# The low parts of fifteen weight tiles move from POOL to DVE in a hybrid attention block

## The chip, the cores and the metric

One core of a Trainium2 chip runs the kernel. The metric is the device time of one execution in microseconds (us); a lower time is better. The kernel before was run three times: 841.33 us median, 840.12 to 841.64.

## The reference, cut to what matters

A decoder block on a sequence of 256 tokens and width 2048 (batch 1, float32): an adaLN-modulated norm, one large input projection, two causal token mixers side by side, a projection for each mixer, a gated merge, an output projection and a sandwich norm.

```python
ada = c @ w_ada + b_ada
shift, scale, gate = split(ada, 3)
h = rms_norm(x, g_pre) * (1 + scale) + shift
proj = h @ w_in                                   # 2048 x 11824
ya = (oa * silu(za)) @ w_br_a                     # 1024 x 2048, oa: sparse attention, 16 heads
yb = (ob * silu(zb)) @ w_br_b                     # 1024 x 2048, ob: dilated attention, 8 heads
merged = sigmoid(ma) * ya + sigmoid(mb) * yb
out = merged @ w_out                              # 2048 x 2048
return x + gate * rms_norm(out, g_post)
```

## The kernel before

Every product with a large weight runs in three parts: a weight tile and an activation are each split into a high part in TensorE's own 32-bit format (fp32r) and a low part, the rest, and high x high, high x low and low x high are summed in PSUM. A weight travels like this. `dma` (L459) loads one item, a tile `raw` of 128 x 1024, from the SP queue; seven such buffers exist. `prep` (L471) makes the high part `wH` with a copy on ACT (L477) and the low part `wL = raw - wH` with a subtraction (L479). There are three buffers of each. `main` (L541) then issues the matmuls through `product` (L518): L535 (wH by the activation's high part), L536 (wH by its low part), L538 (wL by its high part). For an item of two 128-row blocks by 512 columns that is twelve matmuls of 512 columns, six for each half of the tokens.

The items are a list in a fixed order. First come four passes of the input projection; they are not touched by the change. Then come the 32 items of the two branch products (kind `w`, key `br`; four panels of 512 columns, for each panel four items of `w_br_a` and four of `w_br_b`). 32 items of kind `gate` are spread over the end of the projection and over the branch products. A gate item is a 128 x 1024 tile of `w_ada` that DVE multiplies by a column of c and adds to a running sum `gacc` (the first of each half in L497, the others in L499); it has no matmul. Last come the 32 items of the output product (key `out`). `prep` runs three items ahead of `main` (AHEAD).

After the last item of a branch panel, `evac` (L587) merges it on DVE: L619 scales the PSUM result by the gate of its mixer, once for each half of the tokens, and, for the second branch, L622 adds the two mixers' results into `MA`. TensorE then turns that panel's `MA` (L1090, `m_ps`) so that it can be the activation of the output product, ACT and DVE write its high and low parts (L1096, L1097). The gate's sum gets its bias on POOL (L1117), is split and broadcast by TensorE (L1123, L1124) and used at L634 and in the final rows (L1174 to L1188).

The framework's scheduler puts each engine's instructions in order when the program is built, and then every engine works through its own list. That order is not always the order of the source: a loop that writes L619, L622, L619, L622 can be found with another instruction of DVE between its two lines.

The change concerns L478 and L479: `on_pool` is true for an item of kind `w` that doesn't belong to the input projection and whose number in the list is divisible by four. For those, L479 is issued on POOL.

Of the kernel before, what the change touches and what calls it, by code (L numbers as in the profile page):

```python
# [9 lines left out]
F32 = mybir.dt.float32  # L10
# [4 lines left out]
OP = mybir.AluOpType  # L15
# [31 lines left out]
def _build(ctx, tc, x, c, positions, w_ada, b_ada, g_pre, g_post, w_in, pe_ck, pe_cv, w_ck1, w_ck2,  # L47
           w_cv1, w_cv2, w_br_a, w_br_b, w_out, out):
    nc = tc.nc
    V, A, T, G, DMA = nc.vector, nc.scalar, nc.tensor, nc.gpsimd, nc.sync  # L50
# [155 lines left out]
    @contextmanager  # L206
    def behind(*instructions):
        with ExitStack() as st:
            for i in instructions:
                st.enter_context(tc.issue_after(i.ins))  # L210
            yield
# [216 lines left out]
    for n, p in enumerate(panels):  # L428
        a_ = FILL[1] if p[0] in FILLED else 0 if p[0] == "mb" else a
        items += w_job(w_in[0], a_, b, p[1], p[2], (xH, xL), ("proj", 3, 1, p))  # L430
        if n in (3, 4):
            for q in range(4):
                it = Item()
# [11 lines left out]
    for half in range(2):  # L445
        for kt in range(KT):
            it = Item()
# [23 lines left out]
    def prep(i):  # L471
        it = items[i]
        raw = it.raw
        if it.kind in ("w", "ck"):
            H, L = (wp.tile([128, 1024], F32R, name="w" + x, tag="w" + x, bufs=3)[:, :it.nk * it.n].rearrange(
                "p (k n) -> p k n", k=it.nk) for x in "HL")
            A.activation(H, raw, AF.Copy)  # L477
            on_pool = it.kind == "w" and it.jobs[0].key[0] != "proj" and i % 4 == 0  # L478
            (G if on_pool else V).tensor_tensor(L, raw, H.bitcast(F32), op=OP.subtract)  # L479
            it.H, it.L = H, L  # L480
            return
        if it.kind == "ada":
            if it.kt0 == 0:
                accs[it.piece] = ST[:, len(accs) % 2].rearrange("p (h n) -> p h n", h=2)
            acc = accs[it.piece][:, :, :it.n // 2]
        else:
            if it.half not in gacc:
                need("A")
                gacc[it.half] = big.tile([128, 1024], F32, name=f"gacc{it.half}", tag=("cv", "k2")[it.half])
            acc = gacc[it.half]  # L490
        with behind(*(first_h if i < 8 else ())):
            for j in range(it.nk):
                cc, r = cT[:, it.kt0 + j:it.kt0 + j + 1], raw[:, j, :]
                if it.kind == "ada":
                    r = r.rearrange("p (h n) -> p h n", h=2)
                if it.kt0 + j == 0:
                    V.tensor_scalar(acc, r, cc, None, op0=OP.mult)  # L497
                else:
                    V.scalar_tensor_tensor(acc, r, cc, acc, op0=OP.mult, op1=OP.add)  # L499
        if it.fin:  # L500
            if it.kind == "ada":
                fin_ada(it.piece)
            else:
                done.add("gate")

    def fin_ada(piece):
        def gen():
            yield
            make_h(*piece, accs[piece])
            done.add(("h", piece))  # L510
            yield
        side.insert(0, gen())

    def need(*keys):
        while not all(k in done for k in keys):
            side_step(True)
# [631 lines left out]
    def more(i):  # L1148
        prep(i)
        if nxt[0] < n:  # L1150
            dma(nxt[0])
            nxt[0] += 1
# [57 lines left out]
```

## Time and profile before

| | before |
|---|---|
| median of 3 runs | 841.33 us (840.12 to 841.64) |
| the profiled execution | 840.99 us |
| its span | 839.2 us |
| TensorE (PE) busy | 800.3 us, 95% of the span |
| VectorE (DVE) busy | 695.1 us, 83% |
| ScalarE (ACT) busy | 416.4 us, 50% |
| GpSimd (POOL) busy | 135.6 us, 16% |
| mean granted TensorE clock | 0.993 |

The time of the execution is 1.79 us longer than the span, which reaches from the first to the last instruction of the program. Matmuls are pipelined and the records of two neighbours overlap, so a busy PE says only that it has something to do; it is its holes that count here. An instruction's record on DVE or POOL starts when the engine takes it, and can hold time in which it does not yet work on data. Times in the rows are counted from the start of the span.

### The profile page before, as it was taken

To read this page: it belongs to the slowest core of one execution; us is meant where nothing else is said; L and a number is where in the kernel's file an instruction comes from. 1 tells how busy PE (TensorE), PEld (TensorE's weight loads), DVE (VectorE), ACT (ScalarE), POOL (GpSimd) and SP (SyncE) were. 2 spreads that over 40 slices of the span, in tenths; PEclk is the share of its full clock that TensorE was granted. 3 is DMA by queue.
4 is the path that set the end of the run, shared out by engine and by line. 5 is a ranking of instruction groups with operands and counts; after the bars stand their busy time and mean duration, and the time that the engine had idled before them with its cause. 6 is when DMAs were issued, how large, how long until landed. Compare 5 with 4: busy or idle time off the path is not lost.

```text
span 839.2 us, 12023 instructions
## 1 busy us (share of the span) xinstructions
PE 800.3 (95%) x4200; PEld 672.1 (80%) x4200; DVE 695.1 (83%) x1080; ACT 416.4 (50%) x671; POOL 135.6 (16%) x128
## 2 busy tenths in 40 slices
PE   5997999999999999999999999999999989999995
PEld 4785778889887778888888999888888868888884
DVE  4999999999997888898978998777676998855335
ACT  3953263343434446575766666445544433444452
POOL 4200000000000025154311110001003032122221
PEclk9999999999999999999999999999999999999998
DMA  9988899999798547844444545554589989986622
GB/s 313 369 295 262 246 311 291 366 301 325 253 337 295 160 154 227 261 137 128 137 138 116 141 134 158 170 154 145 151 292 322 338 281 324 302 294 196 191 93 100
DMA packets 106663, 193.27 MB, mean 230 GB/s; under 512 B 7561, under 2 KB 36073, under 8 KB 105961
## 3 DMA queue, kind: packets, MB, share of 16 engines
q1 hardware_dynamic: 105088, 189.17, 69.7%
q10 hardware_dynamic: 1514, 3.33, 1.2%
q8 instruction: 33, 0.54, 0.3%
q14 instruction: 28, 0.23, 0.1%
HBM read 190.38 MB, written 2.10 MB: 229 GB/s over the span
## 4 chain that ended last, share of the span: by engine, by line
PE 51%; DVE 4%; issue 1%; ACT 1%; DMA 1%; DVEq 0%; ACTq 0%
PE mm L535 13%; PE mm L536 13%; PE mm L538 13%; PE mm L530 2%; PE mm L525 2%; PE mm L527 2%; DVE wL L479 1%; PE pt_ps L901 1%; PE sA L865 1%; DVE og L1187 1%; PE pvb_ps L1035 1%; PE sB L1025 1%; PE ot_ps L925 1%; PE ot_ps L923 1%; DMA raw<-in_w_ada_dram 1%
## 5 line engine op out<-in xcount | busy, mean ns | idle before, releaser
L477 ACT ACTIVATE wH<-raw 128x1024 fp32r<-128x1024 f32 (+2 forms) x276 | 275.9, 1002 | 326.3 <-PE mm L536 184.0
L479 DVE TENSOR_TENSOR wL<-raw,wH 128x1024 fp32r<-128x1024 f32 (+2 forms) x261 | 309.4, 1191 | 82.9 <-ACT wH L477 80.4
L535 PE MATMUL mm<-wH,xH 128*128 128x512 f32 (+2 forms) x640 | 247.5, 390 | 8.7 <-DVE KB L608 2.5
L536 PE MATMUL mm<-wH,xL 128*128 128x512 f32 (+2 forms) x640 | 245.7, 386 | 0.0
L538 PE MATMUL mm<-wL,xH 128*128 128x512 f32 (+2 forms) x640 | 198.5, 387 | 0.7 <-DVE wL L479 0.6
L535 PEld LDWEIGHTS mm<-wH,xH 128*128 128x128 f32 x640 | 120.2, 188 | 35.1 <-issue 6.1
L538 PEld LDWEIGHTS mm<-wL,xH 128*128 128x128 f32 x640 | 117.7, 188 | 27.7 <-DVE wL L479 2.8
L536 PEld LDWEIGHTS mm<-wH,xL 128*128 128x128 f32 x640 | 120.4, 188 | 23.4 <-DVE xL L237 0.5
L499 DVE SCALAR_TENSOR_TENSOR ST<-raw,vecT,ST 128x768 f32<-128x768 f32 (+2 forms) x75 | 76.3, 1017 | 0.3
L525 PE MATMUL mm<-xH,wH 128*128 128x256 f32 x256 | 67.5, 284 | 1.2 <-DVE VB L608 1.2
L527 PE MATMUL mm<-xL,wH 128*128 128x256 f32 x256 | 66.9, 280 | 0.0
L479 POOL TENSOR_TENSOR wL<-raw,wH 128x1024 fp32r<-128x1024 f32 x15 | 37.6, 2510 | 130.9 <-ACT wH L477 130.9
L530 PE MATMUL mm<-xH,wL 128*128 128x256 f32 x256 | 53.6, 282 | 0.4 <-DVE wL L479 0.4
L535 PE MATMUL mm<-wH,yH 128*128 128x512 f32 x128 | 51.2, 400 | 0.0
L536 PE MATMUL mm<-wH,yL 128*128 128x512 f32 x128 | 51.0, 399 | 0.0
L536 PE MATMUL mm<-wH,mL 128*128 128x512 f32 x128 | 50.8, 397 | 0.0
L535 PE MATMUL mm<-wH,mH 128*128 128x512 f32 x128 | 50.7, 396 | 0.0
L499 DVE SCALAR_TENSOR_TENSOR gacc<-raw,vecT,gacc 128x1024 f32<-128x1024 f32 x30 | 43.9, 1464 | 7.5 <-DMA raw<-in_w_ada_dram 7.4
L525 PEld LDWEIGHTS mm<-xH,wH 128*128 128x128 f32 x256 | 48.0, 188 | 1.9 <-ACT wH L477 1.0
L527 PEld LDWEIGHTS mm<-xL,wH 128*128 128x128 f32 x256 | 48.2, 188 | 0.0
L530 PEld LDWEIGHTS mm<-xH,wL 128*128 128x128 f32 x256 | 40.1, 189 | 1.0 <-DVE wL L479 1.0
L538 PE MATMUL mm<-wL,yH 128*128 128x512 f32 x128 | 40.7, 398 | 0.0
(294 smaller groups left out, 1010.2 us busy)
## 6 DMA issues: line engine op xcount, KB each, us to landing
raw<-in_w_in_dram SPq DMA_DIRECT2D x165, 512.0 KB, 4.4
raw<-in_w_ada_dram SPq DMA_DIRECT2D x48, 512.0 KB, 5.3
raw<-in_w_ada_dram SPq DMA_DIRECT2D x48, 384.0 KB, 4.6
raw<-in_w_out_dram SPq DMA_DIRECT2D x32, 512.0 KB, 4.9
raw<-in_w_br_a_dram SPq DMA_DIRECT2D x16, 512.0 KB, 5.6
raw<-in_w_br_b_dram SPq DMA_DIRECT2D x16, 512.0 KB, 5.4
raw<-in_w_in_dram SPq DMA_DIRECT2D x29, 256.0 KB, 3.0
raw<-in_w_ada_dram SPq DMA_DIRECT2D x24, 256.0 KB, 6.0
```

Source lines behind the costliest of these rows:

```text
L477: A.activation(H, raw, AF.Copy)
L479: (G if on_pool else V).tensor_tensor(L, raw, H.bitcast(F32), op=OP.subtract)
L499: V.scalar_tensor_tensor(acc, r, cc, acc, op0=OP.mult, op1=OP.add)
L525: T.matmul(ps, lhsT=it.H[:, j, bs], rhs=sH[:, it.kt0 + j, :], start=(first and j == 0 and b == 0), stop=False, skip_group_check=True)
L527: T.matmul(ps, lhsT=it.H[:, j, bs], rhs=sL[:, it.kt0 + j, :], start=False, stop=False, skip_group_check=True)
L530: T.matmul(ps, lhsT=it.L[:, j, bs], rhs=sH[:, it.kt0 + j, :], start=False, stop=(last and j == it.nk - 1), skip_group_check=True)
L535: T.matmul(ps, lhsT=sH[:, it.kt0 + j, ts], rhs=it.H[:, j, cs], start=(first and j == 0), stop=False)
L536: T.matmul(ps, lhsT=sL[:, it.kt0 + j, ts], rhs=it.H[:, j, cs], start=False, stop=False)
L538: T.matmul(ps, lhsT=sH[:, it.kt0 + j, ts], rhs=it.L[:, j, cs], start=False, stop=(last and j == it.nk - 1))
L865: T.matmul(o, lhsT=QT[:, u.t, h // 2, h % 2, :], rhs=KTt[:, hl, :, 0:128] if u.t == 0 else KTt[:, hl, u.br, :], start=(hl == 0), stop=(hl ...
L901: T.transpose(ps[:, j, :], u.P[:, j * 128:(j + 1) * 128], ident)
L923: T.matmul(ps, lhsT=vr.rearrange("p l d -> p (l d)"), rhs=u.H[:, :, b, :], start=(first and b == 0), stop=False, skip_group_check=True)
```

## The change

The low part of every weight tile is made on DVE. `on_pool` is gone, and with it the fifteen subtractions on POOL; nothing else is edited.

```diff
@@ -475,8 +475,7 @@
             H, L = (wp.tile([128, 1024], F32R, name="w" + x, tag="w" + x, bufs=3)[:, :it.nk * it.n].rearrange(
                 "p (k n) -> p k n", k=it.nk) for x in "HL")
             A.activation(H, raw, AF.Copy)
-            on_pool = it.kind == "w" and it.jobs[0].key[0] != "proj" and i % 4 == 0
-            (G if on_pool else V).tensor_tensor(L, raw, H.bitcast(F32), op=OP.subtract)
+            V.tensor_tensor(L, raw, H.bitcast(F32), op=OP.subtract)
             it.H, it.L = H, L
             return
         if it.kind == "ada":
```

## Rows read from the trace of the kernel before

**Rows 1.** The page: busy time, share of the span and instructions of each engine, and from the costliest groups the subtraction on POOL (count, then busy us, mean ns of one, idle us before them and what ended it).
```profile
PE 800.3 (95%) x4200; PEld 672.1 (80%) x4200; DVE 695.1 (83%) x1080; ACT 416.4 (50%) x671; POOL 135.6 (16%) x128
...
L479 POOL TENSOR_TENSOR wL<-raw,wH 128x1024 fp32r<-128x1024 f32 x15 | 37.6, 2510 | 130.9 <-ACT wH L477 130.9
```

**Rows 2.** The table by stretches: from and to, length, busy us and (instructions) of PE, PE's weight loads, DVE, ACT and POOL, then the granted clock (1.00 is full), the DMA engines' share and GB/s.
```profile
680.00:685.00 5.00, 5.00 (x23) 4.03 (x22) 4.93 (x5) 1.99 (x2) 1.88 (x2) 1.00 0.64 207
685.00:690.00 5.00, 2.23 (x10) 1.50 (x8) 5.00 (x4) 1.06 (x1) 2.31 (x1) 1.00 0.92 344
690.00:695.00 5.00, 4.07 (x13) 3.33 (x14) 5.00 (x9) 1.72 (x3) 0.50 (x1) 0.66 1.00 371
720.00:730.00 10.00, 10.00 (x45) 8.16 (x44) 9.62 (x12) 4.80 (x6) 0.00 (x0) 1.00 0.90 292
```

**Rows 3.** The timeline of PE around its longest hole of the stretch, later than the start: start, us, line, operation, tiles and shapes, count, and in brackets the idle time before it and what ended it.
```profile
686.84 0.39 PE L538 MATMUL mm<-wL,yH 128*128 128x512 f32 x1
690.93 0.63 PE L1090 MATMUL m_ps<-ident,MA 128*128 128x128 f32 x4 [3.71 <-DVE MA L622]
```

**Rows 4.** The chain that ended last, followed through the stretch from 664 to 700 us: start, us, what.
```profile
678.49 4.29 DMA raw<-in_w_ada_dram
...
683.84 1.22 DVE wL L479
685.06 3.08 DVE gacc L499
...
690.11 0.69 DVE MA L622
...
691.57 0.43 PE mm L535
...
694.98 0.23 PE mm L535
```

**Rows 5.** The hole on PE in the input projection, with no POOL work near it: the timeline of PE, and the table by stretches (columns as in Rows 2).
```profile
74.94 0.47 PE L535 MATMUL mm<-wH,xH 128*128 128x512 f32 x1 [1.73 <-DVE QB L610]
```
```profile
70.00:80.00 10.00, 7.25 (x30) 4.95 (x28) 10.00 (x22) 4.88 (x6) 0.00 (x0) 1.00 0.80 237
```

**Rows 6.** The timeline of POOL from 622 us on.
```profile
646.78 2.39 POOL L479 TENSOR_TENSOR wL<-raw,wH 128x1024 fp32r<-128x1024 f32 x1 [2.64 <-ACT wH L477]
...
678.30 2.43 POOL L479 TENSOR_TENSOR wL<-raw,wH 128x1024 fp32r<-128x1024 f32 x1 [3.46 <-ACT wH L477]
683.85 3.46 POOL L479 TENSOR_TENSOR wL<-raw,wH 128x1024 fp32r<-128x1024 f32 x1 [3.12 <-ACT wH L477]
694.50 2.53 POOL L479 TENSOR_TENSOR wL<-raw,wH 128x1024 fp32r<-128x1024 f32 x1 [7.20 <-ACT wH L477]
701.21 2.41 POOL L479 TENSOR_TENSOR wL<-raw,wH 128x1024 fp32r<-128x1024 f32 x1 [4.18 <-ACT wH L477]
```

**Rows 7.** The timeline of DVE, instructions of the branch products in order of time.
```profile
613.31 0.76 DVE L497 TENSOR_SCALAR gacc<-raw,vecT 128x1024 f32<-128x1024 f32 x1 [1.34 <-DMA raw<-in_w_ada_dram]
...
638.01 1.28 DVE L499 SCALAR_TENSOR_TENSOR gacc<-raw,vecT,gacc 128x1024 f32<-128x1024 f32 x1 [2.68 <-DMA raw<-in_w_ada_dram]
...
644.06 1.23 DVE L479 TENSOR_TENSOR wL<-raw,wH 128x1024 fp32r<-128x1024 f32 x1 [2.18 <-ACT wH L477]
...
647.51 2.75 DVE L499 SCALAR_TENSOR_TENSOR gacc<-raw,vecT,gacc 128x1024 f32<-128x1024 f32 x1 [1.02 <-DMA raw<-in_w_ada_dram]
...
677.24 1.22 DVE L479 TENSOR_TENSOR wL<-raw,wH 128x1024 fp32r<-128x1024 f32 x1
678.38 2.90 DVE L497 TENSOR_SCALAR gacc<-raw,vecT 128x1024 f32<-128x1024 f32 x1
681.32 2.61 DVE L499 SCALAR_TENSOR_TENSOR gacc<-raw,vecT,gacc 128x1024 f32<-128x1024 f32 x2
...
684.98 3.42 DVE L499 SCALAR_TENSOR_TENSOR gacc<-raw,vecT,gacc 128x1024 f32<-128x1024 f32 x1
688.32 0.68 DVE L619 SCALAR_TENSOR_TENSOR MB<-MB,mm 128x512 f32<-128x512 f32 x1
688.91 1.27 DVE L499 SCALAR_TENSOR_TENSOR gacc<-raw,vecT,gacc 128x1024 f32<-128x1024 f32 x1
690.11 0.68 DVE L622 TENSOR_TENSOR MA<-MA,MB 128x512 f32<-128x512 f32 x1
...
694.91 3.21 DVE L499 SCALAR_TENSOR_TENSOR gacc<-raw,vecT,gacc 128x1024 f32<-128x1024 f32 x1
...
701.84 0.69 DVE L619 SCALAR_TENSOR_TENSOR MA<-MA,mm 128x512 f32<-128x512 f32 x1 [0.73 <-PE mm L538]
```

**Rows 8.** The load of a gate item: its issue on the SP queue, and the loads of the stretch from 676 to 692 us (count, KB each, median us from issue to landing).
```profile
682.63 0.34 SPq L467 DMA_DIRECT2D raw<-in_w_ada_dram  x1
```
```profile
raw<-in_w_ada_dram SPq DMA_DIRECT2D x5, 512.0 KB, 5.9
```

**Rows 9.** The next merge of a panel, and the output product: the timeline of DVE (L622), of PE (L1090, and the L538 that uses the tile made by POOL in the third row), and of POOL.
```profile
714.09 0.69 DVE L622 TENSOR_TENSOR MA<-MA,MB 128x512 f32<-128x512 f32 x1
```
```profile
715.11 0.60 PE L1090 MATMUL m_ps<-ident,MA 128*128 128x128 f32 x4
```
```profile
802.35 2.40 POOL L479 TENSOR_TENSOR wL<-raw,wH 128x1024 fp32r<-128x1024 f32 x1 [8.69 <-ACT wH L477]
```
```profile
807.89 0.62 PE L538 MATMUL mm<-wL,mH 128*128 128x512 f32 x2
```

## The prediction

> **What bounds the kernel now.** I read the page first. PE is busy in 95% of the span and DVE in 83%; the fifteen subtractions to be moved take 37.6 us of a POOL that has little else to do [rows 1]. On those shares alone the change looks bad: it takes work from the idle engine and gives it to the second busiest. So I read the table by stretches next, from 630 us on, where the fifteen lie. PE has no hole of note there except one: 2.23 us busy of the five from 685 to 690, and the granted clock falls to a mean of 0.66 in the five that follow [rows 2]. DVE is full in both. The timeline of PE gives the size: the last matmul before the hole begins at 686.84 and ends at 687.23, and the transposes of the merged panel (L1090) wait 3.71 us, until 690.93, for the sum in L622 on DVE [rows 3]. The chain runs through DVE there: wL, gate sum, merge, with a load in front [rows 4].
>
> The clock costs more. From 691.57 to 694.98 matmuls step by 0.43 us, afterwards by 0.23: eight steps at half speed, 1.2 instead of 2.4 GHz, 8 x 0.20 = 1.6, and four transposes of this span 0.63 instead of 0.44, together about 1.7 us [rows 3, 4]. The hole with its slow clock thus costs 3.7 + 1.7 = 5.4 us. Everywhere else in the stage PE is fed, so this is nearly all that an edit here can win. A hole of 1.73 us in the input projection cost no clock: 1.00 in its stretch [rows 5].
>
> **Why DVE is late.** I laid the timelines of POOL and DVE side by side. POOL's subtraction runs from 683.85 to 687.31; the gate sum that DVE took at 684.98 needs 3.42 us and ends at 688.40, 1.1 after POOL. The same form takes 1.27 at 688.91 [rows 6, 7]. The one from 694.91 takes 3.21 beside a POOL subtraction to 697.03, the one from 647.51 2.75 beside one to 649.17; the first of a gate half takes 2.90 from 678.38 beside one to 680.73, and 0.76 at 613.31 with POOL idle [rows 6, 7]. Four of four end about one own length after POOL ends. I read it as: DVE does no work on such an instruction while POOL works. And POOL's own 3.46 at 683.85 holds 1.06 of waiting for a DVE subtraction.
>
> The Trainium skill says the same in its page SBUF — State Buffer (Who interferes with whom): DVE and GpSimd share one pair of ports, and with two SBUF inputs on DVE the second to start is blocked until the first ends. The Trainium skill's page Perfetto Trace Analysis (Optimizing Scalar/DVE Operations) says, against this change, that with a saturated DVE some work may be moved off it, to GpSimd even; in the next sentence it warns that between these two it might not help. By the first sentence the kernel gets slower (rival 3).
>
> **What the change removes and adds.** Each moved subtraction adds one of 1.22 us to DVE, 1.14 from its start to the next start (677.24 to 678.38) [rows 7].
>
> - *Three before the full stretch* (the last is that of 646.78). DVE idles 2.68, 2.18 and 1.02 us there [rows 7]; two additions go into the first two holes, the third costs 1.14 and removes 2.75 - 1.27 = 1.48. Nothing on the path.
> - *Two in the stretch ahead of the hole* (POOL at 678.30 and 683.85). They add 2 x 1.14 = 2.28 and remove 2.90 - 0.76 = 2.14 and 3.42 - 1.27 = 2.15, together 4.29. Net 2.0 us that DVE is earlier.
> - *One or two behind it* (694.50 and 701.21). The first adds 1.14 and removes 3.21 - 1.27 = 1.94. The second adds 1.14 and blocked no DVE instruction: L619 took its ordinary 0.69 [rows 6, 7]. DVE waits 0.73 for PE at that place [rows 7] and so has room.
> - *Eight from 733 on*, the output product. POOL's wL is done at 804.75 there, 3.1 us before L538 needs it at 807.89 [rows 9]. PE has no hole; nothing changes, and on DVE the tile is ready earlier. Should that cover go, each would cost what it is late, at most 1.2.
>
> L1117 stays on POOL, and what it costs DVE is in both kernels.
>
> **The new time of the merge, step by step.** I replay DVE from 677.24 in the order it has now, with the two additions in source order. wL to 678.38; gate start 0.70 to 679.08; added wL (POOL could begin it at 678.30, so its inputs are there [rows 6]) to 680.22; two gate sums of 1.20 to 682.62; wL to 683.76; gate sum to 684.96, whose data land at 682.78 [rows 4], in time; added wL (inputs there by 683.85 [rows 6]) to 686.10; L619 to 686.70. Between L619 and L622 stands a gate sum now [rows 7], so the list is not in source order, and what will fill that place can't be read from this trace. Its load was issued at 682.63, when the buffer of the gate sum from 681.32 came free, and with the median of 5.9 it lands near 688.5 (an estimate) [rows 8]; the sum began at 688.91. In the replay that buffer is free at 681.42, so 1.2 earlier, landing 687.1 to 687.3. Then the sum ends at 688.3 to 688.5. L1090 follows L622's start by 0.82 (690.93 - 690.11). So:
>
> - nothing between: L622 at 686.74, L1090 at 687.56, hole 0.3;
> - a wL of 1.14 between: hole 1.4;
> - the gate sum between: L622 at 688.4, hole 2.0.
>
> Below zero it can't go, as the hole's start is set by PE. I take 1.3, near the middle one, since two of the three fillers are real work. Gain of the hole: 3.71 - 1.3 = 2.4. The clock: a hole of 1.73 kept it [rows 5], one of 3.71 lost it; 0.3 to 2.0 lie at or near the former, so I count the whole 1.7. Sum: 840.99 - 2.4 - 1.7 = 836.9 for a profiled execution. The median of the runs is 0.34 above the profiled one, so 837.2. The bounds 0.3 and 2.0 give 836.2 and 837.9.
>
> **What is late next.** PE comes some 4 us earlier to 701 us, DVE only 2.0 + 0.8 at that place. It has 0.73 there against the 1.14 of the last addition; then it is 9.62 of 10 busy up to 730 [rows 2]. The next merge is tight: L622 ends at 714.78, L1090 starts at 715.11 [rows 9], 0.3 of slack. A miss of 0.5 there would take back 0.5; I keep it for the range.
>
> **The rivals.**
>
> 1. *The hole only shortens and the clock falls all the same* (the gate sum in between waits longer for its load, hole 2 to 3 us). For it: the load is 5.9 us long with the DMA engines 0.92 busy [rows 2, 8]. Gain 3.71 - 2.5 = 1.2, or 840.1; with a hole of 2.0 it is 839.6. Chance 13%.
> 2. *The change does nothing here.* DVE's freed time goes into waits for gate loads: the chain shows one of 4.29 [rows 4], and whichever gate sum is first in the list holds all behind it. Or a new order of the list opens a small hole at another merge. 840.5 to 841.5. Against it: the landing at 682.78 comes before its turn in the replay. Chance 13%.
> 3. *DVE is simply full, and slower.* If the long instructions aren't POOL's doing, the two additions ahead of L622 come on top: 2 x 1.14 = 2.3, hole 6.0, 841.33 + 2.3 = 843.6. It decides at one point: whether a collision costs DVE less than the 1.14 that an addition costs. For it: DVE is full around the hole [rows 2]. Against it: 1.48, 2.14, 2.15 and 1.94 measured, each ended by POOL's end [rows 6, 7]. Chance 12%. The first sentence quoted above from the Trainium skill's Perfetto Trace Analysis would have it so; the four collisions speak for the second.
>
> **How the numbers follow.** The forecast has 62%; of rival 1 half is beyond 0.2% (1.7 us, about what a measurement of this kernel can tell from no change). Faster: 62 + 7 = 69%. Within: 6 + 13 = 19%. Slower: 12%. Likeliest 837.2; its own range is 836.2 to 837.9, widened by the runs' 1.2 below their median. The range of 8 in 10 goes from 835.4 (hole gone, lowest run) to 840.7, which takes in rival 1 and a part of rival 2 and leaves out rival 3.
>
> **What would show it.** Right: POOL has 113 instructions, DVE's gate sums at the merge of the second panel are all near 1.27 and the first of the half 0.76; L622 of that panel lies 2 us or more earlier; PE's hole before L1090 is under 2 us; the clock is 1.00 from 690 to 695. Wrong: DVE instructions of over 2 us remain where POOL has none, or L622 waits behind a gate sum whose load has not landed, or a hole before L1090 at 715 or 740. If the hole is small and the clock still falls, the step on the clock was wrong.

## The result

| | before | changed |
|---|---|---|
| median of 6 runs | 841.49 us (840.12 to 843.69) | 837.25 us (836.89 to 838.74) |
| span of the profiled execution | 839.2 us | 835.5 us |
| DVE busy | 695.1 us | 706.5 us |
| POOL busy | 135.6 us | 97.3 us |

The ratio is 0.995, with a 95% interval from 0.9935 to 0.9965. The kernel is 4.2 us faster, and DVE is busy 11.4 us more than before. Lines of the changed kernel are one less than those of before from L479 on: L478 is the subtraction, L498 the gate sum, L618 and L621 the merge, L1089 the transposes, L1116 the gate's bias.

The page of the changed kernel, busy time of each engine, and the subtraction's group, now all on DVE (count, busy us, mean ns, idle before):

```profile
PE 798.6 (96%) x4200; PEld 671.1 (80%) x4200; DVE 706.5 (85%) x1095; ACT 415.9 (50%) x671; POOL 97.3 (12%) x113
...
L478 DVE TENSOR_TENSOR wL<-raw,wH 128x1024 fp32r<-128x1024 f32 (+2 forms) x276 | 329.1, 1198 | 75.7 <-ACT wH L477 73.0
```

The table by stretches of the changed kernel, columns as in [rows 2]:

```profile
70.00:80.00 10.00, 8.27 (x29) 6.00 (x28) 10.00 (x22) 4.88 (x6) 0.00 (x0) 0.83 0.78 248
...
685.00:690.00 5.00, 3.48 (x19) 2.63 (x17) 4.71 (x7) 1.06 (x1) 0.00 (x0) 1.00 1.00 393
690.00:695.00 5.00, 5.00 (x26) 4.16 (x25) 5.00 (x8) 3.30 (x5) 0.00 (x0) 1.00 1.03 392
```

Set beside [rows 2]: PE has 3.48 busy of the five from 685 to 690 (2.23 before), and the clock is whole in the next five (0.66 before). The timeline of PE gives the hole, to be read against [rows 3]:

```profile
687.66 0.39 PE L535 MATMUL mm<-wH,yL 128*128 128x512 f32 x1
689.57 0.63 PE L1089 MATMUL m_ps<-ident,MA 128*128 128x128 f32 x4 [1.52 <-DVE MA L621]
```

1.52 us in place of 3.71, with the same releaser. And the timeline of DVE ahead of it, to be read line by line against [rows 7]:

```profile
678.78 0.74 DVE L496 TENSOR_SCALAR gacc<-raw,vecT 128x1024 f32<-128x1024 f32 x1
679.55 1.28 DVE L498 SCALAR_TENSOR_TENSOR gacc<-raw,vecT,gacc 128x1024 f32<-128x1024 f32 x1
680.76 1.22 DVE L478 TENSOR_TENSOR wL<-raw,wH 128x1024 fp32r<-128x1024 f32 x1
681.89 1.28 DVE L498 SCALAR_TENSOR_TENSOR gacc<-raw,vecT,gacc 128x1024 f32<-128x1024 f32 x1
683.09 1.22 DVE L478 TENSOR_TENSOR wL<-raw,wH 128x1024 fp32r<-128x1024 f32 x1
684.23 1.28 DVE L498 SCALAR_TENSOR_TENSOR gacc<-raw,vecT,gacc 128x1024 f32<-128x1024 f32 x1
685.43 1.22 DVE L478 TENSOR_TENSOR wL<-raw,wH 128x1024 fp32r<-128x1024 f32 x1
686.56 0.68 DVE L618 SCALAR_TENSOR_TENSOR MB<-MB,mm 128x512 f32<-128x512 f32 x1
687.54 1.28 DVE L498 SCALAR_TENSOR_TENSOR gacc<-raw,vecT,gacc 128x1024 f32<-128x1024 f32 x1 [0.29 <-DMA raw<-in_w_ada_dram]
688.74 0.69 DVE L621 TENSOR_TENSOR MA<-MA,MB 128x512 f32<-128x512 f32 x1
```

The 2.90 has become 0.74 and the 3.42 a 1.28. Three subtractions stand between 680 and 687, where before there was one. A gate sum still stands between the two lines of the merge, and it now waits 0.29 us for its load. The chain of the changed kernel has that load as its largest piece in this stretch (start, us, what); the second line is the ninth matmul behind the transposes:

```profile
680.87 6.57 DMA raw<-in_w_ada_dram
...
692.05 0.45 PE mm L537 x2
```

### The profile page after: what moved, and what is told of

It reads as the page before. It is cut to its first block, busy times and chain, and to the rows that moved or that the text cites. A ratio compares the mean times of both kernels' runs of the same rounds, so it can differ in the third digit from the quotient of the medians.

```text
span 835.5 us, 12016 instructions
## 1 busy us (share of the span) xinstructions
PE 798.6 (96%) x4200; PEld 671.1 (80%) x4200; DVE 706.5 (85%) x1095; ACT 415.9 (50%) x671; POOL 97.3 (12%) x113
## 4 chain that ended last, share of the span: by engine, by line
PE 51%; DVE 4%; issue 1%; DMA 1%; ACT 1%; DVEq 0%
PE mm L534 13%; PE mm L535 13%; PE mm L537 12%; PE mm L529 2%; PE mm L524 2%; PE mm L526 2%; PE pt_ps L900 1%; DVE wL L478 1%; PE sA L864 1%; DMA raw<-in_w_ada_dram 1%; DVE og L1186 1%; PE pvb_ps L1034 1%; PE sB L1024 1%; PE ot_ps L922 1%; PE ot_ps L924 1%
## 5 line engine op out<-in xcount | busy, mean ns | idle before, releaser
L478 DVE TENSOR_TENSOR wL<-raw,wH 128x1024 fp32r<-128x1024 f32 (+2 forms) x276 | 329.1, 1198 | 75.7 <-ACT wH L477 73.0
L498 DVE SCALAR_TENSOR_TENSOR ST<-raw,vecT,ST 128x768 f32<-128x768 f32 (+2 forms) x75 | 76.9, 1025 | 0.3
L498 DVE SCALAR_TENSOR_TENSOR gacc<-raw,vecT,gacc 128x1024 f32<-128x1024 f32 x30 | 38.4, 1282 | 3.2 <-DMA raw<-in_w_ada_dram 2.9
L537 PE MATMUL mm<-wL,mH 128*128 128x512 f32 x128 | 39.8, 390 | 0.0
```

Of the source, the lines that this page charges most:

```text
L478: V.tensor_tensor(L, raw, H.bitcast(F32), op=OP.subtract)
L537: T.matmul(ps, lhsT=sH[:, it.kt0 + j, ts], rhs=it.L[:, j, cs], start=False, stop=(last and j == it.nk - 1))
```

## The experiments

Each was run beside the kernel before. The ratio is to that kernel on the same chip. The theory: an instruction of POOL that reads tiles holds up DVE instructions that meet it, for as long as POOL runs; two such collisions ahead of the second panel's merge made the hole.

**Only the two subtractions ahead of the hole on DVE.** The edit, set against the changed kernel:

```diff
+    fifteen = []
...
+            on_pool = it.kind == "w" and it.jobs[0].key[0] != "proj" and i % 4 == 0
+            if on_pool:
+                fifteen.append(i)
+            on_pool = on_pool and len(fifteen) not in (4, 5)
-            V.tensor_tensor(L, raw, H.bitcast(F32), op=OP.subtract)
+            (G if on_pool else V).tensor_tensor(L, raw, H.bitcast(F32), op=OP.subtract)
```

> Of the fifteen subtractions only the two ahead of the hole (on POOL from 678.30 and 683.85 us in the kernel before) go to DVE; thirteen stay on POOL. Theory (the gain is DVE freed of two collisions with POOL ahead of the second panel's merge): hole before L1090 near 1.5 us as in the changed kernel, 837.2 to 838.2 us, the rest because the collision near 694 stays. Rival (the gain is spread over the fifteen, 4.2 / 15 = 0.28 us each): 840.9 us with the hole near 3.2.

838.4 us, ratio 0.9969 (0.996 to 0.9979), 0.2 us above the expected range. The hole at the merge is 1.52 us as in the changed kernel, and over one us of the gain is missing. The timelines of PE, DVE and POOL of this kernel show where (L1095 are the transposes, L504 the gate sum, L1102 the low part behind the transposes, L484 the subtraction):

```profile
695.63 0.63 PE L1095 MATMUL m_ps<-ident,MA 128*128 128x128 f32 x4 [1.63 <-DVE mL L1102]
```
```profile
692.07 3.22 DVE L504 SCALAR_TENSOR_TENSOR gacc<-raw,vecT,gacc 128x1024 f32<-128x1024 f32 x1
695.21 0.28 DVE L1102 SCALAR_TENSOR_TENSOR mL<-m_ps,mH 128x128 fp32r<-128x128 f32 x1
```
```profile
691.81 2.39 POOL L484 TENSOR_TENSOR wL<-raw,wH 128x1024 fp32r<-128x1024 f32 x1 [16.66 <-DVE MA L627]
```

The third collision is still there, and with PE earlier it now makes a hole of its own, 1.63 us. In the changed kernel it is gone with the others. So two of fifteen bring most of it, 2.6 us. That the third brings the rest is read from this hole; no run moved it by itself.

**Only these two on POOL, the other thirteen on DVE** (`len(fifteen) in (4, 5)`).

> The reverse: the two ahead of the hole stay on POOL, the other thirteen go to DVE. Theory: the hole is 3 to 4 us again and DVE shows two instructions of 2.9 and 3.4 us ahead of it, 840.5 to 842 us. Rival (the gain is spread): 841.5 - 13 x 0.28 = 837.8 us.

841.34 us, ratio 1.0002 (0.9992 to 1.0011): no gain at all. PE's holes in this kernel:

```profile
688.07 0.73 PE L543 MATMUL mm<-wL,yH 128*128 128x512 f32 x2 [0.55 <-DVE wL L484]
691.75 1.06 PE L1095 MATMUL m_ps<-ident,MA 128*128 128x128 f32 x4 [2.95 <-DVE MA L627]
```

0.55 and 2.95, together 3.5, and the clock fell again. Thirteen moved subtractions are worth nothing by themselves.

**Both engines make the low part.** POOL's copy goes into a scratch tile in bfloat16 that nobody reads.

```diff
             V.tensor_tensor(L, raw, H.bitcast(F32), op=OP.subtract)
+            if it.kind == "w" and it.jobs[0].key[0] != "proj" and i % 4 == 0:
+                sc = work.tile([128, 1024], BF, name="sc", tag="sc", bufs=1)[...]
+                G.tensor_tensor(sc, raw, H.bitcast(F32), op=OP.subtract)
```

> DVE makes all fifteen low parts as in the changed kernel, and POOL makes each a second time into a scratch tile (bfloat16) that nobody reads; the collisions are there without work being taken from DVE. Theory (a collision costs DVE the time that POOL runs): DVE is late by 2 x 2.15 = 4.3 us at the merge against the changed kernel, hole 1.5 + 4.3 = 5.8 us, clock lost, 837.25 + 4.3 + 1.7 = 843.3 us. Rival (how much work DVE has decides, not what POOL does beside it): 837.3 us.

848.49 us, ratio 1.0095 (1.008 to 1.011). DVE's own work is that of the changed kernel, and it is 11.2 us slower. It went the expected way, and further than expected. DVE ahead of the second merge, and PE's holes (L1093 are the transposes):

```profile
681.31 2.90 DVE L500 TENSOR_SCALAR gacc<-raw,vecT 128x1024 f32<-128x1024 f32 x1
...
687.78 3.42 DVE L478 TENSOR_TENSOR wL<-raw,wH 128x1024 fp32r<-128x1024 f32 x1
```
```profile
665.60 0.74 PE L1093 MATMUL m_ps<-ident,MA 128*128 128x128 f32 x4 [2.09 <-DVE MA L625]
...
691.26 0.74 PE L541 MATMUL mm<-wL,yH 128*128 128x512 f32 x2 [1.46 <-DVE wL L478]
...
696.08 1.09 PE L1093 MATMUL m_ps<-ident,MA 128*128 128x128 f32 x4 [3.61 <-DVE MA L625]
...
722.04 0.63 PE L1093 MATMUL m_ps<-ident,MA 128*128 128x128 f32 x4 [1.74 <-DVE MA L625]
```

The second merge loses 1.46 + 3.61 = 5.1 us, near the 5.8 expected. What I hadn't counted are the merges before and behind it: with additions and collisions at once the first and third lose 2.09 and 1.74, and the clock fell after the first too. POOL's second copy also keeps `raw` and `wH` in use for longer; how much of the 11.2 us that makes, no run separates. Here a 1.22 subtraction pays with 3.42, where in [rows 7] the gate sum paid. So it is not one kind of instruction that is held up. Not all are, though: in the kernel before, L619 (at 701.84 [rows 6, 7]) and L1097 (at 694.71), which read one input from PSUM, keep their 0.69 and 0.28 us beside a subtraction on POOL.

**POOL busy in the same places, but reading nothing.**

```diff
             V.tensor_tensor(L, raw, H.bitcast(F32), op=OP.subtract)
+            if it.kind == "w" and it.jobs[0].key[0] != "proj" and i % 4 == 0:
+                sc = work.tile([128, 512], F32, name="sc", tag="sc", bufs=1)
+                A.activation(sc[:, 0:1], H[:, 0, 0:1], AF.Copy)
+                for _ in range(4):
+                    G.memset(sc, 0.0)
```

> As the changed kernel, and after each of the fifteen high parts POOL sets a scratch tile of 128 x 512 four times to zero (a tiny copy on ACT ties it to the high part): POOL is busy at the same places and reads no memory. Theory (DVE and POOL share the way by which POOL reads): DVE's lengths stay at 1.22 and 1.28, 837.3 us. Rival (any work of POOL holds DVE up): DVE instructions of over 2 us and 840 to 843 us.

836.84 us, ratio 0.9953 (0.9939 to 0.9968): the time of the changed kernel. POOL, then DVE beside it:

```profile
678.40 2.81 POOL L483 MEMSET sc<- 128x512 f32 x4 [3.68 <-ACT sc L481]
683.94 2.28 POOL L483 MEMSET sc<- 128x512 f32 x4 [2.73 <-ACT sc L481]
```
```profile
679.03 1.28 DVE L503 SCALAR_TENSOR_TENSOR gacc<-raw,vecT,gacc 128x1024 f32<-128x1024 f32 x1
680.23 1.22 DVE L478 TENSOR_TENSOR wL<-raw,wH 128x1024 fp32r<-128x1024 f32 x1
...
684.89 1.22 DVE L478 TENSOR_TENSOR wL<-raw,wH 128x1024 fp32r<-128x1024 f32 x1
```

POOL works 2.81 and 2.28 us where it worked 2.43 and 3.46 before, and DVE's instructions keep 1.22 and 1.28. So it isn't POOL's being busy that holds DVE up, but its reading. The Trainium skill states just this (SBUF — State Buffer, Who interferes with whom): two inputs in SBUF contend with a GpSimd instruction that reads SBUF, not with one that only writes. The trace agrees on both halves.

**The fifteen subtractions on neither engine.** For these items the third product takes the high part a second time in place of the low part, which is left out; PE's work is the same.

```diff
+            if it.kind == "w" and it.jobs[0].key[0] != "proj" and i % 4 == 0:
+                it.H, it.L = H, H
+                return
             V.tensor_tensor(L, raw, H.bitcast(F32), op=OP.subtract)
```

> The fifteen subtractions are made on neither engine: for those items the high part stands in the third product in place of the low part, so part of the result's low-order digits is left out; TensorE does the same work. Theory (what is left of the hole, 1.5 us, waits for the load of the gate sum between the two lines of the merge): DVE is 2.3 us less loaded at the merge, but the hole stays 1 to 1.5 us, 836.6 to 837.3 us, and DVE shows idle time ended by a load there. Rival (the additions on DVE are on the path): hole gone, 835.7 us.

837.04 us, ratio 0.9944 (0.9929 to 0.996), no faster than the changed kernel. The hole is 1.88 us, larger even, as the two matmuls that stand ahead of the transposes in the changed kernel come behind them here. DVE, 2.3 us less loaded here, waits for loads instead (L501 is the gate sum):

```profile
683.92 1.28 DVE L501 SCALAR_TENSOR_TENSOR gacc<-raw,vecT,gacc 128x1024 f32<-128x1024 f32 x1 [1.54 <-DMA raw<-in_w_ada_dram]
...
686.52 1.28 DVE L501 SCALAR_TENSOR_TENSOR gacc<-raw,vecT,gacc 128x1024 f32<-128x1024 f32 x1 [0.72 <-DMA raw<-in_w_ada_dram]
```

1.54 + 0.72 = 2.26 of waiting, where the changed kernel waits 0.29: nearly all of what the two missing additions set free. In the changed kernel these two additions cost next to nothing: they fill time in which DVE would wait for gate loads. The clock fell here, after a hole of 1.88.

**The gate's bias on DVE as well.**

```diff
-            G.tensor_tensor(ga[0:1, :], ga[0:1, :], bg[:, half * 1024:(half + 1) * 1024], op=OP.add)
+            V.tensor_tensor(ga[0:1, :], ga[0:1, :], bg[:, half * 1024:(half + 1) * 1024], op=OP.add)
```

> As the changed kernel, and the gate's bias (L1116, on POOL from 672.8 us) goes to DVE too, so that no collision is left in the branch products. DVE loses the 3.29 us subtraction at 673 (2.07 over its length) and gains one addition of about 1.2 us. Theory (each collision ahead of the merge costs what POOL runs, and the gate sum's load goes out earlier with DVE): hole 0 to 0.7 us, 835.8 to 836.5 us. Rival (this collision is made up for by 687 us): hole 1.5, 837.2 us.

The collision that this takes away, in the changed kernel (POOL, then DVE):

```profile
672.84 2.41 POOL L1116 TENSOR_TENSOR gacc<-gacc,bg 1x1024 f32<-1x1024 f32 x1 [81.25 <-DVE gacc L498]
```
```profile
673.04 3.29 DVE L478 TENSOR_TENSOR wL<-raw,wH 128x1024 fp32r<-128x1024 f32 x1
```

834.7 us, ratio 0.9917 (0.9904 to 0.9929): better than either kernel and than the 835.8 that I had as the lower bound. The transposes follow without a hole, and DVE's list has changed at the merge: a subtraction stands between its lines, and no gate sum. So this run changes the collision and the order at once, and by itself it doesn't tell the two apart.

```profile
687.39 0.60 PE L1089 MATMUL m_ps<-ident,MA 128*128 128x128 f32 x4
```
```profile
684.71 0.68 DVE L618 SCALAR_TENSOR_TENSOR MB<-MB,mm 128x512 f32<-128x512 f32 x1
685.31 1.22 DVE L478 TENSOR_TENSOR wL<-raw,wH 128x1024 fp32r<-128x1024 f32 x1
686.44 0.69 DVE L621 TENSOR_TENSOR MA<-MA,MB 128x512 f32<-128x512 f32 x1
```

**Nothing between the merge's lines.** An order is written in: later gate sums and subtractions stay behind L621 of the first half.

```diff
+                    m = V.tensor_tensor(da, da, d, op=OP.add)
+                    if t == 0:
+                        first_half[:] = [m]
...
+            with behind(*first_half):
+                V.tensor_tensor(L, raw, H.bitcast(F32), op=OP.subtract)
...
+        with behind(*(first_h if i < 8 else first_half)):
```

> As the changed kernel, with an order written in: on DVE the gate sums and subtractions that come later in the source stay behind L621 of a panel's first half, so that nothing stands between the merge's two lines. Theory (the gate sum between L618 and L621, with 0.3 us of waiting for its load, is what is left of the hole): L621 1.2 to 1.5 us earlier, hole 0 to 0.3 us, 835.7 to 836.3 us. Rival (something else on DVE, or PE's own order, holds L1089): 837.2 us.

835.85 us, ratio 0.9932 (0.992 to 0.9945). The two lines stand together (L620 and L623 here), and PE has no hole before these transposes; one of 0.55 us has come up at the fourth panel.

```profile
684.30 0.69 DVE L620 SCALAR_TENSOR_TENSOR MB<-MB,mm 128x512 f32<-128x512 f32 x1
685.03 0.69 DVE L623 TENSOR_TENSOR MA<-MA,MB 128x512 f32<-128x512 f32 x1
```

**Both of these edits together.**

> The two edits before together: the bias on DVE and nothing between the merge's two lines. Theory (the hole can't go below zero): no more than either alone, hole 0 to 0.2 us, 835.6 to 836.2 us. Rival (the two gains add up): 834.5 us.

834.59 us, ratio 0.9917 (0.9902 to 0.9932): a us below the expected range and at the rival's price, but no different from the bias alone (834.7), so the gains don't add: each by itself already closes the hole. That can't be the whole of the bias edit's gain, though. It is 1.15 us faster than the ordered merge, and every run of the one is below every run of the other; the hole of 0.55 at the fourth panel is a part of this, and the rest stays open.

**Single steps on the kernel before.** First the bias alone on DVE, with all fifteen left on POOL; then one subtraction alone on DVE, that of 678.30 (`len(fifteen) != 4`).

> The kernel before with one edit: the gate's bias (L1117) on DVE; all fifteen subtractions stay on POOL. Theory (collisions ahead of the merge add up, each for itself): 2.07 us saved, 1.2 added, DVE 0.9 us earlier with the collisions of 678 and 684 left, hole 2.8 us, the clock falls as before, 0.9 us under the kernel before: about 840.6 us. Rival (the bias was the cause by itself): 835 to 837 us.

> Only one subtraction goes to DVE, the one that ran on POOL from 678.30 us; fourteen stay on POOL. Theory: 2.14 saved, 1.14 added, hole 3.71 - 1.0 = 2.7 us; the clock falls as it did after 2.95 and 3.71: about 840.5 us. Rival (this one collision alone sets the hole): 837.3 us as with both.

839.11 us, ratio 0.9977 (0.9967 to 0.9987), and 839.84 us, ratio 0.9978 (0.9967 to 0.999). The holes, bias first:

```profile
690.40 0.87 PE L1090 MATMUL m_ps<-ident,MA 128*128 128x128 f32 x3 [2.74 <-DVE MA L622]
```
```profile
691.18 0.63 PE L1095 MATMUL m_ps<-ident,MA 128*128 128x128 f32 x4 [2.66 <-DVE MA L627]
```

2.74 and 2.66 where the theory had 2.8 and 2.7; the clock fell in both profiled executions. Each collision has its own price of about one us of hole, net of the work that DVE takes over, and none is the cause by itself. The times are 1.8 and 1.0 us under the 840.87 of the kernel before that ran beside them. The first is more than the 1.0 us by which the hole shrank (3.71 to 2.74), and the runs scatter, those of the second from 836.8 to 841.25. A part of it goes with the clock: three runs of the first and two of the second have a mean granted clock of 0.997, which none of the kernel before's 53 runs beside the experiments reaches (0.990 to 0.995), and they took 837.9 to 838.6 us. The rest stays open.

## Why the prediction was right, step by step

- *What bounds it.* Right. PE's one hole and its clock were where the time was; thirteen of the moved subtractions are worth nothing while the two ahead of the hole stay on POOL (841.34), and moving those two alone gives 838.4. But the 5.4 us of hole and clock were not "nearly all that an edit here can win": with the bias on DVE too, the kernel is 6.9 us faster than the one before (841.57 beside 834.7).
- *Why DVE is late.* Right, and shown from both sides: with the collisions kept and the work moved, 848.49; with POOL as busy but not reading, 836.84.
- *Net 2.0 us for DVE ahead of the merge.* Right. The changed kernel's profile has this stretch 0.38 later (the collision with the bias starts at 673.04, not 672.66). Less that, the first line of the merge begins at 686.18 where it was 688.32, 2.1 earlier. The replay had L622 at 688.4 for the case of a gate sum in between; it is at 688.74, so at 688.36.
- *The filler.* Of the three cases the third came, a gate sum that waits for its load, with a bound of 2.0 us of hole; I had put 1.3. It is 1.52, because PE's list too changed: the transposes stand two matmuls later, some 0.45 us, and so the hole began later. The prediction had taken PE's side as fixed. That 1.3 came out near 1.52 is luck: DVE did what the case of 2.0 says, and a change on PE's side, which the prediction didn't have, made up for it.
- *The clock.* It came back, as 1.6 us and not 1.7. From the start of the transposes to the ninth matmul behind them it was 694.98 - 690.93 = 4.05 us [rows 3, 4], and is 692.05 - 689.57 = 2.48. The 0.19 that I had counted for the transposes was no matter of the clock: four take 0.63 in the changed kernel too, at 1.00. And the ground for the step was weak. I took a hole of 1.73 in the input projection as proof that such a one costs no clock [rows 5]. In the changed kernel's profile the same hole, 1.73 us long, is followed by half speed: 0.83 in the stretch from 70 to 80. It cost nothing there, as DVE is full in that stretch: PE stands at the same point 9.31 us behind the end of the hole (84.03 - 74.72), 9.32 before (84.26 - 74.94). With 1.88 the clock fell in the experiment that leaves the work out. So that it stayed whole after 1.52 was luck as far as the prediction goes.
- *What is late next.* Half right. The merge of the third panel did not open a hole. But I had counted the collision of 694 only as time that DVE gains, 0.8 us; it would have cost a hole of 1.63 as soon as PE came earlier, as the run with only two on DVE shows. The change takes it away, so the sum did not suffer.
- *The sum.* 837.2 against 837.25; 4.1 us of gain against 4.24. In the profiled executions the hole gave 2.2 and the clock 1.6, together 3.8, where they differ by 840.99 - 837.32 = 3.7; the rest up to the 4.2 of the medians is less than the runs scatter. Agreement to 0.05 us is therefore luck, with a hole of 1.3 for 1.52 and a clock of 1.7 for 1.6 in it; that a gain of this size came, and from the collisions, is not.
- *The signs.* POOL's 113 instructions, DVE's lengths, the hole under 2 us and the whole clock came as listed. Two signs went the other way: L622's place is 1.4 us earlier (690.11 to 688.74; 1.75 without the shift of 0.38) and not 2 or more, and it waits behind a gate sum whose load had not landed, which was on the list of what would show the prediction wrong. The cause is the filler: the wait was only 0.29 us, so it cost little. This is what rival 1 described, with a wait too short for its price.
- *Rivals.* DVE was full, as rival 3 had it, and is fuller now; that did not decide. The sentence of the Trainium skill's Perfetto Trace Analysis (Optimizing Scalar/DVE Operations) on moving work off a saturated DVE fails here by its price: the move to POOL spared DVE 1.14 us and cost it up to 2.15. Its next sentence, that it might not help between these two, holds.

## What to carry to other kernels

Where POOL and DVE both read tiles in the same stretch, compare an instruction's length with the same form elsewhere: a 1.27 that is sometimes 3.4 isn't slow, it is held up, and the hold-up ends with an instruction of POOL. Here that held for instructions that read tiles in SBUF alone, not for those with an input in PSUM. Work given to the idle engine then has a price on the busy one, and it should be counted there before the shares of busy time are believed. And an engine's busy time may rise with a faster kernel: what matters is which instruction stands ahead of the one that the bounding engine waits for.

## What was not expected of the hardware

The clock after a hole of PE: it fell to half after holes of 3.71, 3.61, 2.95, 2.74, 2.66, 2.09 and 1.88 us, and stayed whole after 1.10, 1.52 and 1.63. At 1.72 to 1.74 it went either way. Every kernel here has such a hole in the input projection, near 74 us: after it the clock fell in three of twelve profiled executions (the changed kernel, the one without the fifteen subtractions, the one with the merge kept whole) and stayed whole in nine; after 1.74 at 722 us, with both engines at work, it stayed whole. So the same hole in the same place can be followed by either clock from one execution to the next.

The length of a hold-up doesn't go by how much POOL's instruction computes: the gate's bias, 1x1024 on a single partition, takes POOL 2.41 us, as long as a tile of 128x1024, and makes DVE's subtraction take 3.29. POOL is held up too: the 3.46 of [rows 6], and the first of four memsets at 678.40 beside DVE's tensor by scalar at 678.25 (four took 2.81 there, 2.28 at 683.94).
